# Low parts of the projection weights on another engine: GpSimd in place of DVE

## The chip, the cores and the metric

The kernel runs on one core of one Trainium2 chip. The core has five engines that matter here, each with an instruction stream of its own that it works off in order: TensorE (PE in the profile; its weight loads are PEld), VectorE (DVE), ScalarE (ACT), GpSimd (POOL) and SyncE (SP), which issues most of the transfers from device memory. The metric is the device time of one execution in microseconds (us). The kernel before was timed three times: 902.83, 899.54 and 899.51 us, median 899.54 us.

## The reference, cut to what matters

One block of a transformer for 512 tokens of width 1024, in fp32: `h = h + mixer(rmsnorm(h))`, then attention to 256 memory rows, then a gated feed-forward, then a last norm. The mixer is where the change lies. It projects the normed input `u` (512 x 1024) with one wide weight matrix and feeds three attention branches:

```
p = split_columns(u @ w_in)
o_a = stick_breaking(q_a, k_a, v_a)                                  # 4 heads
o_b = dsa(rope(q_b), rope(k_b), v_b, rope(q_idx), rope(k_idx), w_idx)  # top 128 of the keys
o_c = nsa(rope(q_c), rope(k_cmp), v_cmp, rope(k_sel), v_sel, rope(k_win), v_win, gates, ...)
g = sigmoid(g_merge)
merged = g[0]*(o_a @ w_up[0]) + g[1]*(o_b @ w_up[1]) + g[2]*(o_c @ w_up[2])
```

## The kernel before, in words

**Products in two parts.** TensorE works on a rounded form of fp32. To come near full fp32 the kernel writes each operand as a sum of a high part (the value rounded, made by a cast) and a low part (what the rounding left, made by a subtraction), and sums three products: high by high, low by high, high by low (`mm3`, L94 to L96). Every weight tile is therefore loaded by SP into a tile `raw` (128 x 1024 at most), cast on ACT into `whi` (L58), and subtracted into `wlo = raw - whi` (L66). `ring` (L71 to L87) makes such a loader for a pool: `load_split` has three buffers of each tile and subtracts on DVE, `load_fill` has two and subtracts on GpSimd. Both subtractions stand on the same line, L66, and are told apart in the profile by the engine.

**Stages.** The order in time is: the norm and the projections of branch a (0 to 54 us of the profiled execution); the stick-breaking heads of branch a (54 to 106 us), in which TensorE fills its waits with matmuls of three merge gates (tiles `gf`); the later projections (106 to 195 us); the attentions of branches c and b with the top-k search on DVE (195 to 300 us); the merge gates, the memory attention and the feed-forward.

**The later projections.** `project` (L231) is called five times: for 256 columns of keys and values of branch c (`post_g2`, two weight tiles of 4 x 256 columns), for 336 columns in three pieces (`post_g1`, weight tiles of 1008, 1008 and 672 columns), and for the queries of the indexer, of branch c and of branch b (`post_q`, two weight tiles each; in the texts below qi, qc and qb). That is eleven weight tiles. For each of four chunks of 128 tokens it accumulates 24 matmuls into a bank `gm`, ACT copies the bank to `p` (L228), and DVE applies the rotary embedding with `p` and a table `cst` (L244 to L246). For the keys GpSimd makes a second copy of each rotated row (`rk`, L299) and copies value columns (L458 to L461, L445, L446). For the queries ACT casts the rotated rows into `stk` and DVE subtracts their low part into `stk` as well (L58, L66). TensorE then transposes `rk` or `stk` (L253, L466) one or two chunks later: these transposes are put into a list `late` and issued after the matmuls of a following chunk. Between qi and qc, and between qc and qb, stand the matmuls of a compression (tiles `av`), whose weights come through `load_fill`.

**What sets the order.** The program is written as one sequence, and a scheduler in the tile layer then orders the instructions of each engine by its own estimates. On the chip each engine takes its list in order: an instruction that waits holds up all that stand behind it on the same engine. The order is thus fixed before the run, and a change of engine can move other instructions too.

Of the kernel before, what the change touches and what calls it, by code (L numbers as in the profile page):

```python
# [18 lines left out]
NK = D // P  # L19
# [7 lines left out]
def block_kernel(ctx: ExitStack, tc: tile.TileContext, A, out, dbg=None):  # L27
    nc = tc.nc
# [42 lines left out]
    def ring(pl, bufs, hi_eng=None, lo_eng=None):  # L71

        def load(shape, parts, lo_eng=lo_eng):
            n = shape[0] * shape[1]
            raw = pl.tile([P, WT], F32, name="raw", bufs=bufs[0])
            rv = raw[:, :n].rearrange("p (k n) -> p k n", n=shape[1])
            off = 0
            for src in parts:
                w = src.shape[-1]
                nc.sync.dma_start(rv[:, :, off:off + w], src)  # L80
                off += w
            hi = pl.tile([P, WT], F32R, name="whi", bufs=bufs[1])
            lo = pl.tile([P, WT], F32R, name="wlo", bufs=bufs[1])
            split(hi[:, :n], lo[:, :n], raw[:, :n], hi_eng, lo_eng)
            return [t[:, :n].rearrange("p (k n) -> p k n", n=shape[1]) for t in (hi, lo)]
        return load

    load_split = ring(stage, (3, 3))
# [14 lines left out]
    def col_view(w, c0, n):  # L103
        return w.rearrange("(k p) n -> p k n", p=P)[:, :, c0:c0 + n]
# [62 lines left out]
    def load_half(ranges, k0, kn, load):  # L167
        hi, lo = load((kn, sum(w for _, w in ranges)), [col_view(w_in, c0, w)[:, k0:k0 + kn, :] for c0, w in ranges])
        return [(hi[:, k, :], lo[:, k, :]) for k in range(kn)]
# [52 lines left out]
    def project_chunk(c, n, tiles, post, keep=0):  # L222
        acc = gm_ps.tile([P, 512], F32, name=up_tag[gm_ps is gf_ps])
        for k in range(NK):
            ins = mm3(acc[:, :n], (uT[0][:, k, cc(c)], uT[1][:, k, cc(c)]), tiles[k], k == 0, k == NK - 1)
        flush(ins, keep)
        p = pw.tile([P, 336], F32, name="p", bufs=2)
        nc.scalar.copy(p[:, :n], acc[:, :n])  # L228
        late.append(post(c, p))

    def project(ranges, kstep, post, keep=0):  # L231
        n = sum(w for _, w in ranges)
        tiles = [t for k0 in range(0, NK, kstep) for t in load_half(ranges, k0, min(kstep, NK - k0), load_split)]
        for c in range(NT):
            project_chunk(c, n, tiles, post, keep)

# [261 lines left out]
    def compressed(hid):  # L498
# [23 lines left out]
        nc.vector.tensor_copy(vc, res[0:32, 64:128])  # L522

    project([(1732, 256)], 4, post_g2)
    project([(1024, 128), (1408, 68), (1988, 140)], 3, post_g1)
    blk = [blocks_of(cmp_t[0], A["cmp_pos_k"][0]), blocks_of(cmp_t[1], A["cmp_pos_v"][0])]
    hid = av_ps.tile([P, 2, P], F32, name="av")
    project([(1152, 256)], 4, post_q(qi, 1.0), 1)
    compress(0, blk[0], A["cmp_w1_k"][0], hid)
    project([(1476, 256)], 4, post_q(qc, 0.125), 1)  # L530
# [395 lines left out]
```

## Time and profile before

| what | value |
|---|---|
| median of the three timed runs | 899.54 us |
| profiled execution | 898.28 us, its span 896.5 us |
| TensorE busy | 856.3 us, 96% of the span |
| DVE busy | 507.8 us, 57% |
| ACT busy | 411.5 us, 46% |
| GpSimd busy | 140.7 us, 16% |
| granted TensorE clock, mean | 0.994 of full speed |

The profile comes from one execution that took 898.28 us, 1.26 us less than the median of the timed runs; 1.78 us of it lie outside the profiled span. Start times are counted from the span's start. A row of the timeline gives the start, the duration, the engine, the line, the operation, the tiles (output, arrow, inputs), their shapes, a count where equal instructions are drawn together, and in brackets the idle time ahead of it with what ended that. Line numbers are those of the kernel before; behind L233 the changed kernel's are higher by 2.

### The profile page before, as it was taken

How to read it: one execution, taken by the hardware profiler on the slowest of the kernel's cores; microseconds unless marked ns; L12 is line 12 of the kernel's file. 1: busy time of each engine (PE TensorE's matmuls, PEld its weight loads, DVE VectorE, ACT ScalarE, POOL GpSimd, SP SyncE). 2: the span in 40 equal slices, each digit the busy share in tenths (PEclk: the TensorE clock that was granted, in tenths of full speed). 3: DMA queues.
4: the chain of work that ended last, by engine and by line, in shares of the span. 5: the costliest groups of instructions: out<-in, count | busy, mean ns of one | idle time of the engine just before them, and what ended most of it. 6: DMA issues, size and time to landing. Idle time of an engine off the chain costs nothing.

```text
span 896.5 us, 13084 instructions
## 1 busy us (share of the span) xinstructions
PE 856.3 (96%) x5012; PEld 731.7 (82%) x5012; DVE 507.8 (57%) x1155; ACT 411.5 (46%) x779; POOL 140.7 (16%) x116
## 2 busy tenths in 40 slices
PE   5999999899989999999989999999999999999995
PEld 5987899787757788978878979988888888888884
DVE  4456378799998305676677758643443334322226
ACT  6487545557774224544654545432322333211123
POOL 4021232302211347430232010000000000000002
PEclk9999999999999999999999999999999999999998
DMA  9340124510210334558446514642333332333312
GB/s 323 85 110 24 43 58 119 141 48 24 70 26 24 95 94 141 187 174 246 125 150 199 165 49 142 187 142 94 97 102 105 97 94 94 118 94 95 99 42 94
DMA packets 93710, 99.00 MB, mean 110 GB/s; under 512 B 4656, under 2 KB 81616, under 8 KB 93648
## 3 DMA queue, kind: packets, MB, share of 16 engines
q1 hardware_dynamic: 91568, 92.75, 34.0%
q10 hardware_dynamic: 2080, 5.42, 1.9%
q8 instruction: 39, 0.64, 0.3%
q14 instruction: 23, 0.19, 0.1%
HBM read 96.06 MB, written 2.10 MB: 109 GB/s over the span
## 4 chain that ended last, share of the span: by engine, by line
PE 85%; DVE 7%; ACT 4%; issue 2%; DMA 1%; POOL 0%; ACTq 0%; DVEq 0%; POOLq 0%
PE wo L95 9%; PE wo L96 9%; PE wo L94 9%; PE gf L94 6%; PE gf L95 6%; PE gf L96 6%; PE ff L94 4%; PE ff L95 4%; PE ff L96 4%; PE gm L94 3%; PE gm L95 3%; PE gm L96 3%; PE y L96 2%; PE y L94 2%; PE y L95 2%; PE av L101 2%
## 5 line engine op out<-in xcount | busy, mean ns | idle before, releaser
L58 ACT CAST whi<-raw 128x1024 fp32r<-128x1024 f32 (+1 forms) x167 | 174.8, 1048 | 292.4 <-PE y L96 78.9
L66 DVE TENSOR_TENSOR wlo<-raw,whi 128x1024 fp32r<-128x1024 f32 (+1 forms) x131 | 164.1, 1255 | 211.2 <-ACT whi L58 210.9
L66 POOL TENSOR_TENSOR wlo<-raw,whi 128x1024 fp32r<-128x1024 f32 x36 | 88.9, 2474 | 312.9 <-ACT whi L58 267.1
L95 PE MATMUL wo<-ut_lo,whi 128*128 128x256 f32 (+1 forms) x320 | 105.2, 329 | 0.0
L96 PE MATMUL wo<-ut_hi,wlo 128*128 128x256 f32 (+1 forms) x320 | 104.6, 327 | 0.0
L94 PE MATMUL wo<-ut_hi,whi 128*128 128x256 f32 (+1 forms) x320 | 104.4, 326 | 0.0
L96 PE MATMUL gf<-ut_hi,wlo 128*128 128x512 f32 (+1 forms) x192 | 69.8, 363 | 0.0
L94 PE MATMUL gf<-ut_hi,whi 128*128 128x512 f32 (+1 forms) x192 | 69.3, 361 | 0.0
L95 PE MATMUL gf<-ut_lo,whi 128*128 128x512 f32 (+1 forms) x192 | 69.3, 361 | 0.0
L94 PE MATMUL ff<-ut_hi,whi 128*128 128x512 f32 (+1 forms) x192 | 67.9, 354 | 0.0
L95 PE MATMUL ff<-ut_lo,whi 128*128 128x512 f32 (+1 forms) x192 | 67.9, 354 | 0.0
L96 PE MATMUL ff<-ut_hi,wlo 128*128 128x512 f32 (+1 forms) x192 | 67.9, 354 | 0.0
L95 PEld LDWEIGHTS wo<-ut_lo,whi 128*128 128x128 f32 x320 | 60.9, 190 | 6.2 <-issue 1.0
L94 PEld LDWEIGHTS wo<-ut_hi,whi 128*128 128x128 f32 x320 | 60.8, 190 | 5.8 <-issue 0.7
L96 PEld LDWEIGHTS wo<-ut_hi,wlo 128*128 128x128 f32 x320 | 60.8, 190 | 5.6 <-issue 0.4
L875 POOL TENSOR_TENSOR ut_hi<-ut_hi,ut_lo 128x512 f32<-128x512 f32 x4 | 5.0, 1276 | 367.0 <-ACT ut_hi L874 367.0
L94 PE MATMUL gm<-whi,ut_hi 128*128 128x256 f32 (+1 forms) x160 | 47.4, 296 | 0.0
L95 PE MATMUL gm<-wlo,ut_hi 128*128 128x256 f32 (+1 forms) x160 | 46.4, 290 | 0.0
L96 PE MATMUL gm<-whi,ut_lo 128*128 128x256 f32 (+1 forms) x160 | 46.3, 289 | 0.0
L96 PEld LDWEIGHTS gf<-ut_hi,wlo 128*128 128x128 f32 x192 | 36.2, 188 | 5.6 <-issue 1.2
L95 PEld LDWEIGHTS gf<-ut_lo,whi 128*128 128x128 f32 x192 | 36.2, 188 | 5.4 <-issue 0.8
L94 PEld LDWEIGHTS gf<-ut_hi,whi 128*128 128x128 f32 x192 | 36.2, 188 | 5.3 <-issue 0.8
(329 smaller groups left out, 2027.7 us busy)
## 6 DMA issues: line engine op xcount, KB each, us to landing
raw<-in_w_ffn_in_dram SPq DMA_DIRECT2D x56, 512.0 KB, 3.6
raw<-in_w_in_dram SPq DMA_DIRECT2D x46, 512.0 KB, 3.9
raw<-in_w_ffn_out_dram SPq DMA_DIRECT2D x22, 512.0 KB, 3.5
raw<-in_w_out_dram SPq DMA_DIRECT2D x16, 512.0 KB, 3.6
raw<-in_w_up_dram SPq DMA_DIRECT2D x8, 512.0 KB, 4.0
xt<-in_x_dram SPq DMA_DIRECT2D x4, 512.0 KB, 9.0
raw<-in_w_mem_kv_dram SPq DMA_DIRECT2D x4, 512.0 KB, 3.8
raw<-in_w_mem_q_dram SPq DMA_DIRECT2D x4, 512.0 KB, 3.8
```

The costliest lines, as they stand in the source:

```text
L58: nc.scalar.copy(dst, src)
L66: (lo_eng or nc.vector).tensor_sub(dst_lo, src, dst_hi.bitcast(F32))
L94: nc.tensor.matmul(dst, lh, rh, start=first, stop=False, skip_group_check=True)
L95: nc.tensor.matmul(dst, lh, rl, start=False, stop=False, skip_group_check=True)
L96: return nc.tensor.matmul(dst, ll, rh, start=False, stop=last, skip_group_check=True).ins
L101: nc.tensor.matmul(dst[64 * x:64 * x + 64], lhs[x], rhs[x], start=first, stop=last, skip_group_check=True)
L875: nc.gpsimd.tensor_mul(yo[:, n], yo[:, n], gain[:, n])
```

## The change

`project` gets its weight tiles through a loader that is `load_split` with the subtraction on GpSimd. The three buffers, the casts on ACT and the transfers stay. The other users of `load_split` keep DVE.

```
+    load_proj = lambda *a: load_split(*a, lo_eng=nc.gpsimd)
+
     def project(ranges, kstep, post, keep=0):
         n = sum(w for _, w in ranges)
-        tiles = [t for k0 in range(0, NK, kstep) for t in load_half(ranges, k0, min(kstep, NK - k0), load_split)]
+        tiles = [t for k0 in range(0, NK, kstep) for t in load_half(ranges, k0, min(kstep, NK - k0), load_proj)]
         for c in range(NT):
             project_chunk(c, n, tiles, post, keep)
```

Eleven instructions leave DVE's list and eleven enter GpSimd's. SP's list is the same. TensorE's list differs only in where some `gf` matmuls stand among those of the stick-breaking heads; from the first later projection on it is the same. ACT's list differs at two places, where instructions change places with near neighbours.

GpSimd's list at the end of branch a's projections, before. `wlo_1124`, `wlo_1157` and `wlo_1190` belong to the three merge gates that fill the stick-breaking stage, `wlo_2022` and `wlo_2052` to the first compression:

```order
L66 TENSOR_TENSOR wlo_136<-raw_133,whi_135 128x1024
L66 TENSOR_TENSOR wlo_142<-raw_139,whi_141 128x1024
L66 TENSOR_TENSOR wlo_1124<-raw_1121,whi_1123 128x1024
L66 TENSOR_TENSOR wlo_1157<-raw_1154,whi_1156 128x1024
L66 TENSOR_TENSOR wlo_1190<-raw_1187,whi_1189 128x1024
L66 TENSOR_TENSOR wlo_2022<-raw_2019,whi_2021 128x1024
```

The same place now. `wlo_1267` and `wlo_1273` are the tiles of `post_g2`, `wlo_1507` is the first of `post_g1`:

```order
L66 TENSOR_TENSOR wlo_136<-raw_133,whi_135 128x1024
L66 TENSOR_TENSOR wlo_142<-raw_139,whi_141 128x1024
L66 TENSOR_TENSOR wlo_1267<-raw_1264,whi_1266 128x1024
L66 TENSOR_TENSOR wlo_1273<-raw_1270,whi_1272 128x1024
L66 TENSOR_TENSOR wlo_1124<-raw_1121,whi_1123 128x1024
L66 TENSOR_TENSOR wlo_1157<-raw_1154,whi_1156 128x1024
L66 TENSOR_TENSOR wlo_1507<-raw_1502,whi_1506 128x1008
L66 TENSOR_TENSOR wlo_1190<-raw_1187,whi_1189 128x1024
```

Two subtractions stand ahead of the first two gates' and one behind them.

GpSimd's list where `post_g2` ends and `post_g1` begins, before (copies for the fourth chunk of `post_g2`):

```order
L299 COPY rk_1433<-rk_1433 128x64
L458 COPY vv_1489<-p_1478 128x64
L459 COPY vv_1489<-p_1478 128x64
L461 COPY vsel_1241<-p_1478 128x64
L299 COPY rk_1480<-rk_1480 128x64
L299 COPY rk_1492<-rk_1492 128x64
```

The same place now, with the second and third tile of `post_g1` (`wlo_1515`, `wlo_1523`):

```order
L301 COPY rk_1433<-rk_1433 128x64
L66 TENSOR_TENSOR wlo_1515<-raw_1510,whi_1514 128x1008
L460 COPY vv_1489<-p_1478 128x64
L461 COPY vv_1489<-p_1478 128x64
L463 COPY vsel_1241<-p_1478 128x64
L66 TENSOR_TENSOR wlo_1523<-raw_1518,whi_1522 128x672
L301 COPY rk_1480<-rk_1480 128x64
L301 COPY rk_1492<-rk_1492 128x64
```

The three copies stand between the two subtractions, and the last two copies behind both.

GpSimd's list from the end of `post_g1` to the second compression (`wlo_2266`, `wlo_2296`), before:

```order
L299 COPY rk_1714<-rk_1714 128x64
L299 COPY rk_1723<-rk_1723 128x64
L445 COPY vb_1240<-p_1774 128x64
L446 COPY vwin_1242<-p_1774 128x64
L299 COPY rk_1776<-rk_1776 128x64
L299 COPY rk_1785<-rk_1785 128x64
L299 COPY rk_1794<-rk_1794 128x64
L66 TENSOR_TENSOR wlo_2266<-raw_2263,whi_2265 128x1024
```

The same place now, with the tiles of qi (`wlo_1840`, `wlo_1846`), of qc (`wlo_2082`, `wlo_2088`) and the first of qb (`wlo_2411`):

```order
L301 COPY rk_1714<-rk_1714 128x64
L66 TENSOR_TENSOR wlo_1840<-raw_1837,whi_1839 128x1024
L301 COPY rk_1723<-rk_1723 128x64
L66 TENSOR_TENSOR wlo_1846<-raw_1843,whi_1845 128x1024
L447 COPY vb_1240<-p_1774 128x64
L448 COPY vwin_1242<-p_1774 128x64
L301 COPY rk_1776<-rk_1776 128x64
L66 TENSOR_TENSOR wlo_2082<-raw_2079,whi_2081 128x1024
L301 COPY rk_1785<-rk_1785 128x64
L301 COPY rk_1794<-rk_1794 128x64
L66 TENSOR_TENSOR wlo_2088<-raw_2085,whi_2087 128x1024
L66 TENSOR_TENSOR wlo_2411<-raw_2408,whi_2410 128x1024
```

Three subtractions stand among the `rk` copies that TensorE's transposes read, and two ahead of the second compression's. The last moved one, `wlo_2417` of qb, stands behind `wlo_2296`.

## Rows read from the trace of the kernel before

**Rows 1.** The page's first part: busy time and share of each engine.
```profile
PE 856.3 (96%) x5012; PEld 731.7 (82%) x5012; DVE 507.8 (57%) x1155; ACT 411.5 (46%) x779; POOL 140.7 (16%) x116
```
**Rows 2.** The page's fourth part: engines on the chain that ended last.
```profile
PE 85%; DVE 7%; ACT 4%; issue 2%; DMA 1%; POOL 0%; ACTq 0%; DVEq 0%; POOLq 0%
```
**Rows 3.** Busy time by stretch: length, engines, clock, DMA share, GB/s.
```profile
134.00:146.00 12.00, 11.19 (x90) 10.55 (x89) 11.98 (x45) 6.31 (x16) 3.24 (x6) 1.00 0.31 90
146.00:158.00 12.00, 12.00 (x127) 12.00 (x126) 9.05 (x19) 7.59 (x13) 3.98 (x2) 1.00 0.46 137
...
260.00:270.00 10.00, 6.87 (x42) 4.37 (x41) 9.73 (x33) 6.44 (x15) 2.37 (x1) 0.93 0.20 53
```
**Rows 4.** DVE by line and shape, 40 to 196 us: busy us, mean ns, idle before.
```profile
L66 DVE TENSOR_TENSOR wlo<-raw,whi 128x1024 fp32r<-128x1024 f32 x11 | 13.4, 1223 | 2.5 <-ACT whi L58 2.5
...
L66 DVE TENSOR_TENSOR wlo<-raw,whi 128x1008 fp32r<-128x1008 f32 x2 | 3.7, 1853 | 1.2 <-ACT whi L58 1.2
```
**Rows 5.** GpSimd in order of time, 80 to 160 us.
```profile
82.44 2.56 POOL L66 TENSOR_TENSOR wlo<-raw,whi 128x1024 fp32r<-128x1024 f32 x1 [26.77 <-ACT whi L58]
...
119.26 0.23 POOL L461 COPY vsel<-p 128x64 f32<-128x64 f32 x1
...
133.91 1.10 POOL L299 COPY rk<-rk 128x64 f32<-128x64 f32 x1 [0.51 <-DVE rk L246]
...
154.02 4.81 POOL L66 TENSOR_TENSOR wlo<-raw,whi 128x1024 fp32r<-128x1024 f32 x2 [14.55 <-ACT whi L58]
```
**Rows 6.** DVE in order of time, 54 to 161 us.
```profile
54.24 2.49 DVE L66 TENSOR_TENSOR wlo<-raw,whi 128x1008 fp32r<-128x1008 f32 x1 [0.64 <-ACT whi L58]
56.77 0.42 DVE L66 TENSOR_TENSOR ka_lo<-ps,ka_hi 128x256 fp32r<-128x256 f32 x1
...
59.01 0.69 DVE L60 CAST sph<-sbs 128x512 fp32r<-128x512 f32 x2
...
83.71 1.38 DVE L60 CAST sph<-sbs 128x128 fp32r<-128x128 f32 x1
...
144.20 0.42 DVE L66 TENSOR_TENSOR stk<-t,stk 128x256 fp32r<-128x256 f32 x1
...
156.49 2.48 DVE L245 TENSOR_TENSOR t<-p,cst 128x128 f32<-128x128 f32 x1
158.90 0.28 DVE L244 TENSOR_TENSOR t<-p,cst 128x128 f32<-128x128 f32 x1
...
160.36 0.43 DVE L66 TENSOR_TENSOR stk<-t,stk 128x256 fp32r<-128x256 f32 x1 [0.53 <-ACT stk L58]
```
**Rows 7.** TensorE in order of time, 57 to 171 us.
```profile
57.25 0.33 PE L96 MATMUL ps<-qa_hi,ka_lo 128*128 128x128 f32 x1 [0.71 <-DVE ka_lo L66]
...
119.86 0.31 PE L95 MATMUL gm<-wlo,ut_hi 128*128 128x336 f32 x1
...
121.35 0.42 PE L95 MATMUL gm<-wlo,ut_hi 128*128 128x336 f32 x1
...
135.06 0.33 PE L253 MATMUL ps<-cst,rk 128*128 128x128 f32 x1 [0.35 <-POOL rk L299]
...
145.41 0.60 PE L253 MATMUL ps<-cst,stk 128*128 128x128 f32 x4
...
161.57 0.60 PE L253 MATMUL ps<-cst,stk 128*128 128x128 f32 x4
...
170.26 0.66 PE L253 MATMUL ps<-cst,stk 128*128 128x128 f32 x4 [1.46 <-DVE stk L66]
```
**Rows 8.** ACT in order of time, 46 to 153 us.
```profile
46.88 1.05 ACT L58 CAST whi<-raw 128x1024 fp32r<-128x1024 f32 x1 [0.65 <-PE gf L96]
...
116.76 1.03 ACT L58 CAST whi<-raw 128x1008 fp32r<-128x1008 f32 x1
...
132.37 1.05 ACT L58 CAST whi<-raw 128x1024 fp32r<-128x1024 f32 x1
...
152.58 0.41 ACT L58 CAST stk<-t 128x256 fp32r<-128x256 f32 x1 [1.68 <-DVE t L246]
```

## The prediction

> **What bounds the kernel now.** I read the page's busy shares first: TensorE is busy 96% of the span, DVE 57%, GpSimd 16% [rows 1]. On shares alone GpSimd has room and DVE does not need any. The chain that ended last agrees: 85% of it is TensorE, 7% DVE and nothing to speak of GpSimd [rows 2]. So TensorE's list, taken in order, sets the time, and a change counts by what it adds to or takes from TensorE's waits. A share is a mean over stages, so the busy times by stretch come next: from 134 to 146 us DVE is busy 11.98 of 12 us, while TensorE works 11.19 [rows 3]. There the two run neck and neck, and it is in the middle of the stage that is changed. Last I read the timelines of DVE, GpSimd, TensorE and ACT through 46 to 175 us [rows 5 to 8], for who ends whose wait and by how much.
>
> **What one moved subtraction costs.** A 128 x 1024 subtraction takes 1.22 us on DVE [rows 4] and 2.40 us on GpSimd (two in 4.81 us, the row at 154.02) [rows 5]. Eight of 1024 columns, two of 1008 and one of 672 move. DVE is rid of 8 x 1.22 + 3.7 + 0.8 = 14.3 us (0.8 being 1.22 x 672/1024). GpSimd gets 2.40 x (8 x 1024 + 2 x 1008 + 672)/1024 = 25.5 us. Neither sum is on TensorE's path by itself.
>
> The two engines do not run freely beside each other. The rotary product at 156.49 us, with both inputs in SBUF, took 2.48 us, and the next of the same shape 0.28 us; it lay beside the second GpSimd subtraction of the pair 154.02 to 158.83 and ended with it [rows 5, 6]. The cast of 128 columns at 83.71 us took 1.38 us and ended where GpSimd's subtraction of 82.44 ended, at 85.0 [rows 5, 6]. The other way round, the 64-column copy on GpSimd at 133.91 took 1.10 us [rows 5], where the like of it takes 0.23 (119.26). So I count a moved subtraction as 2.40 us in which DVE's rotary products, low parts of `stk` and SBUF casts stand still, against 1.22 us of DVE work saved: a loss of 1.18 us for DVE wherever it has no idle time. Between two subtractions one DVE instruction gets through, as in the pair at 154.02.
>
> The Trainium skill, page "SBUF — State Buffer", section "Who interferes with whom", has this as a rule: a DVE instruction with two SBUF inputs contends with a GpSimd instruction that reads SBUF, and whoever issues first blocks the other fully. By that rule, the trace agrees, the blocked terms below count in full; if the two merely shared the port, only the waits for the low parts themselves would be left, which is the first rival.
>
> **Term 1, the start of the stick-breaking heads.** TensorE waits 0.71 us at 57.25 for `ka_lo` [rows 7]. `ka_lo` came only at 56.77 because the 1008-column subtraction of 54.24 to 56.73 stood ahead of it on DVE, twice its length beside GpSimd's gates [rows 6]. That goes: -0.71. Late next is the cast of `sph` at 59.01 [rows 6]. GpSimd now has five subtractions in a row from 47.93 (46.88 + 1.05, the end of the first cast [rows 8]), to 47.93 + 5 x 2.40 = 59.9 us. The cast waits until then, 0.9 us or more. TensorE, 0.71 earlier, would want it at about 59.3 and gets it at about 60.3: +1.0. Net +0.3; bounds -0.7 (the cast slips in) and +0.6 (another DVE instruction goes between two subtractions).
>
> **Term 2, the second and third tile of `post_g1`.** The cast of the second ends at 117.79 [rows 8], its subtraction on GpSimd at 117.79 + 2.36 = 120.15. TensorE wants it at 119.86 [rows 7]: +0.3. Three copies of 0.23 us stand between [rows 5], then the third tile's 1.58 us: 120.15 + 0.7 + 1.58 = 122.4 at the earliest, against 121.35 [rows 7]; where each copy lets a rotary product through first, 122.8 to 123.1. Bounds +1.05 and +1.75, I take +1.4; the 0.3 is inside it.
>
> **Term 3, qi.** The first cast ends at 133.42 [rows 8], the subtraction at 135.82, and only behind it comes the copy of `rk_1723`, to about 136.15. TensorE's transpose had it at 135.06 [rows 7]: +1.1. Behind it DVE, without idle time here [rows 3], is blocked by `wlo_1840`, `wlo_1846` and `wlo_2082`: 3 x 2.40 = 7.2 us, less the two subtractions that it made itself before this point, 2.4: 4.8 us late. The low part of `stk` for the first transposes of qi ended at 144.20 + 0.42 = 144.62, TensorE wanted it at 145.41 [rows 6, 7], 0.8 of slack. So +4.0 at that transpose, the 1.1 included. Bounds: +1.05 if the rotary products slip in between, +5.0 if nothing does.
>
> **Term 4, qc.** `wlo_2088` and `wlo_2411` block 4.8 us; DVE is rid of three subtractions by then, 3.7 us, and 9.05 of 12 us busy leave a little room [rows 3]. Slack at the first transposes of qc is 161.57 - 160.79 = 0.8 us [rows 6, 7]. That alone is +0.3. But the two casts of the second compression stand on ACT behind the cast of `stk` that already waited 1.68 us for DVE at 152.58 [rows 8]; a late DVE makes those casts late, and their two GpSimd subtractions then fall on the rotary products of qc with less room than at 156.49. Fully late that is +3.2. Bounds 0 and +3.2, I take the middle, +1.6.
>
> **Term 5, the last transposes of qc.** TensorE waits 1.46 us at 170.26 for `stk` [rows 7], behind two DVE subtractions. One of them (`wlo_2417`) goes, 1.2 us, and blocks up to 2.4 us from GpSimd instead, +1.2 at most and -1.2 if it blocks nothing. I take +0.8, near the upper end, because the row at 156.49 blocked in full, and a little is hidden while the first product waits for its `p`.
>
> At nothing I cost the three `raw` buffers that come free later, since TensorE's waits in these stretches end on DVE, ACT or GpSimd and none on a weight transfer, and everything behind 195 us, where no instruction changed; the attentions start when qb is done, so the delay is carried to the end. If that cover failed, it would cost up to the 1.2 us by which a `raw` buffer is held longer.
>
> **Sum.** 0.3 + 1.4 + 4.0 + 1.6 + 0.8 = +8.1 us on the profiled execution of 898.28: 906.4 us. The median of the timed runs stood 1.26 us above that execution, so I forecast 907.6 us.
>
> **Rivals.**
> First, only the waits for low parts count, and DVE's products slip in between GpSimd's work. For it: one did at 154.02 to 156.5. Against: the next one stood still for 2.48 us. Terms: -0.7 + 1.05 + 1.1 = about +1.5, to 899.8, or 901 as a median.
>
> Second, not slower: DVE, at 11.98 of 12 us, is the true bound of the stage, and the work taken from it ends TensorE's waits. What would go is 0.71 at 57.25, 0.35 at 135.06 and 1.46 at 170.26 [rows 7], 2.5 us: 895.8, or 897 as a median; faster than that only if the queries' chain shortens too. It decides if GpSimd's subtractions run so early that their blocking falls into DVE's idle time. For it: DVE has three quarters of its time busy behind 146 us, not all [rows 3]. Against: the cast of qi's first tile ends at 133.42 [rows 8], 1.6 us ahead of the transpose that stands before its use [rows 7], less than one subtraction of 2.40.
>
> Third, dearer: all upper bounds, 0.6 + 1.75 + 5.0 + 3.2 + 1.2 = 11.75 us, and a lower clock on top. From 260 to 270 us, with TensorE busy 6.87 of 10, the granted clock was 0.93 [rows 3]; at that, 40 us cost 2.8 us more. 898.28 + 14.5 + 1.26 = 914.
>
> That the change does not do what it says is excluded by the lists: eleven instructions changed engine.
>
> **How the numbers follow.** The forecast has 0.60 (904 to 912 us), the first rival 0.16, the second 0.10, the third 0.14. About 0.5%, 4.5 us, is what a measurement of this kernel can tell from no change: faster is under 895.0, slower over 904.0. Slower gets the forecast and the third, 0.74. Same gets the first and half of the second, 0.21. Faster gets the other half, 0.05. The range of 900 to 915 us holds the forecast, the first rival and most of the third, and leaves out the second and a worse third.
>
> **What would show it.** Right: TensorE waits with a releaser on GpSimd at the first chunk of `post_g1` and at the transposes of the last `rk` of its third chunk; a wait of 2 us or more for `stk` at the first transposes of qi; rotary products of 2 us or more on DVE between 118 and 175 us; the 0.71 us for `ka_lo` gone. Wrong: no such long rotary product beside a moved subtraction, or TensorE's idle time from 118 to 175 us not grown by over 3 us. The whole is wrong if the projections end (about 195 us) no later than before, or if a difference arises behind them.

## The result and the profile after

The changed kernel took 909.75 us (median of 4 runs, 908.94 to 910.47), the kernel before 899.52 us in the runs beside it. The ratio is 1.0114, with a 95% interval of 1.0099 to 1.0128: slower by 10.2 us. The profiled execution's span is 908.5 us, 12.0 us more than before. Below, line numbers are the changed kernel's (2 more than before behind L233); an experiment's are its own.

The first and the fourth part of the page, to be held against [rows 1, 2]:

```profile
PE 862.6 (95%) x5012; PEld 736.2 (81%) x5012; DVE 513.2 (56%) x1144; ACT 411.0 (45%) x779; POOL 163.9 (18%) x127
...
PE 80%; DVE 9%; ACT 5%; issue 2%; DMA 2%; POOL 1%; SPq 0%; ACTq 0%; DVEq 0%; POOLq 0%
```

GpSimd gained 23.2 us of busy time (140.7 to 163.9). Its weight subtractions alone gained 25.3 (36 in 88.9 us before, 47 in 114.2 now); 25.5 were worked out. DVE was rid of eleven subtractions and 14.3 us, yet its busy time rose by 5.4 us: an instruction that stands still for GpSimd is drawn as a long one. TensorE's share of the chain fell from 85% to 80%, DVE's rose from 7% to 9%.

TensorE in order of time, those rows that begin with a wait (in brackets; what ended it behind the arrow), for [rows 7]:

```profile
59.70 0.51 PE L342 MATMUL ps<-sph,fixed 128*128 128x512 f32 x1 [1.09 <-DVE sph L60]
...
84.84 0.44 PE L342 MATMUL ps<-sph,fixed 128*128 128x128 f32 x2 [1.45 <-DVE sph L60]
...
121.89 0.42 PE L95 MATMUL gm<-wlo,ut_hi 128*128 128x336 f32 x1 [0.26 <-POOL wlo L66]
...
124.00 0.42 PE L95 MATMUL gm<-wlo,ut_hi 128*128 128x336 f32 x1 [0.45 <-POOL wlo L66]
...
125.87 0.33 PE L468 MATMUL ps<-cst,rk 128*128 128x128 f32 x1 [0.62 <-POOL rk L301]
...
139.82 0.33 PE L255 MATMUL ps<-cst,rk 128*128 128x128 f32 x1 [1.62 <-POOL rk L301]
...
152.53 0.66 PE L255 MATMUL ps<-cst,stk 128*128 128x128 f32 x4 [1.25 <-DVE stk L66]
...
171.18 0.95 PE L255 MATMUL ps<-cst,stk 128*128 128x128 f32 x4 [2.28 <-DVE stk L66]
...
181.26 0.66 PE L255 MATMUL ps<-cst,stk 128*128 128x128 f32 x4 [1.27 <-DVE stk L66]
...
186.97 0.45 PE L294 MATMUL ps<-ki_hi,qi 128*128 128x384 f32 x1 [1.78 <-ACT rel L546]
```

The wait for `ka_lo` at 57.25 is gone. Three short waits for GpSimd are new in `post_g1`, the one for the last `rk` of its third chunk grew from 0.35 to 1.62 us, and the first transposes of qi (152.53) and of qc (171.18) now wait for DVE, which they did not. The last wait of 1.78 us stood before too, in the kernel before at 176.48:

```profile
172.19 0.39 PE L292 MATMUL ps<-ki_hi,qi 128*128 128x256 f32 x1 [0.56 <-ACT qc L260]
...
176.48 0.44 PE L292 MATMUL ps<-ki_hi,qi 128*128 128x384 f32 x1 [1.78 <-ACT rel L544]
```

GpSimd in order of time:

```profile
47.37 11.99 POOL L66 TENSOR_TENSOR wlo<-raw,whi 128x1024 fp32r<-128x1024 f32 x5 [28.20 <-ACT whi L58]
...
137.01 2.37 POOL L66 TENSOR_TENSOR wlo<-raw,whi 128x1024 fp32r<-128x1024 f32 x1
139.53 0.24 POOL L301 COPY rk<-rk 128x64 f32<-128x64 f32 x1
...
143.82 2.41 POOL L66 TENSOR_TENSOR wlo<-raw,whi 128x1024 fp32r<-128x1024 f32 x1 [0.38 <-ACT whi L58]
...
157.03 4.81 POOL L66 TENSOR_TENSOR wlo<-raw,whi 128x1024 fp32r<-128x1024 f32 x2 [9.59 <-ACT whi L58]
164.37 4.79 POOL L66 TENSOR_TENSOR wlo<-raw,whi 128x1024 fp32r<-128x1024 f32 x2 [2.54 <-ACT whi L58]
```

DVE in order of time:

```profile
58.38 1.53 DVE L60 CAST sph<-sbs 128x512 fp32r<-128x512 f32 x2
...
137.06 2.40 DVE L248 TENSOR_TENSOR rk<-t,t 128x64 f32<-128x64 f32 x1
...
143.90 2.57 DVE L247 TENSOR_TENSOR t<-p,cst 128x32 f32<-128x32 f32 x2
...
157.25 2.33 DVE L246 TENSOR_TENSOR t<-p,cst 128x128 f32<-128x128 f32 x1 [0.79 <-ACT p L228]
159.50 2.48 DVE L247 TENSOR_TENSOR t<-p,cst 128x128 f32<-128x128 f32 x1
...
165.54 1.37 DVE L246 TENSOR_TENSOR t<-p,cst 128x128 f32<-128x128 f32 x1 [1.74 <-ACT p L228]
166.84 2.48 DVE L247 TENSOR_TENSOR t<-p,cst 128x128 f32<-128x128 f32 x1
```

Lay the two lists side by side. The subtraction of 137.01 ends at 139.38; DVE's sum into the last `rk`, a 64-column operation that takes 0.21 us elsewhere, starts at 137.06 and ends at 139.46; the copy of `rk` follows at 139.53 and TensorE has it at 139.82. The pair of 157.03 (the second tile of qc and the first of qb) covers two rotary products, the pair of 164.37 two more. That second pair is the compression's, which GpSimd made before the change too [rows 5]; it now comes 10.35 us later and falls on the rotary products of qc's first chunk.

Where the delay arises, from TensorE's timelines of both kernels (start of the first projection, ends of the transposes, end of the last matmul):

| place | before | after | late by | added there |
|---|---|---|---|---|
| first projection starts | 105.84 | 107.45 | 1.61 | 1.61 |
| `post_g1`, second chunk | 130.78 | 134.28 | 3.50 | 1.89 |
| `post_g1`, third chunk | 135.39 | 140.15 | 4.76 | 1.26 |
| qi, first chunk | 146.01 | 153.19 | 7.18 | 2.42 |
| qc, first chunk | 162.17 | 172.13 | 9.96 | 2.78 |
| qc, last chunk | 170.91 | 181.92 | 11.01 | 1.05 |
| qb, first chunk | 187.59 | 199.43 | 11.84 | 0.83 |
| last matmul | 885.9 | 897.9 | 12.0 | 0.2 |

All of it arises ahead of 200 us. The first row holds a difference that is not the change's: TensorE waited 1.35 us at 19.85 us in the kernel before and 0.71 us at 19.22 in the changed one, each time for a low part of branch a's projections, which the change does not touch. From there to 52 us, ahead of anything that was moved, the changed kernel's execution lay 0.64 us in front. From 52 us to the first projection it thus lost 2.25 us. Busy time by stretch of the changed kernel shows one thing more (the number ahead of the last two is the granted clock):

```profile
86.00:90.00 4.00, 4.00 (x17) 3.52 (x16) 2.13 (x4) 3.12 (x8) 0.00 (x0) 0.57 0.42 125
140.00:144.00 4.00, 4.00 (x21) 3.90 (x21) 3.66 (x18) 1.76 (x5) 2.87 (x5) 0.59 0.62 164
172.00:176.00 4.00, 4.00 (x25) 4.00 (x25) 2.48 (x8) 2.48 (x5) 0.00 (x0) 0.65 0.04 12
188.00:192.00 4.00, 4.00 (x15) 3.30 (x14) 3.58 (x6) 2.68 (x6) 0.00 (x0) 0.57 0.35 106
```

Four times the clock was for the most part at its lower level (1.2 instead of 2.4 GHz), each time behind one of the waits of 1.45, 1.62, 2.28 and 1.78 us above. In the kernel before it stayed at 1.00 there, and behind its own 1.78 us too:

```profile
140.00:144.00 4.00, 4.00 (x36) 4.00 (x35) 4.00 (x13) 2.30 (x6) 0.00 (x0) 1.00 0.04 11
172.00:176.00 4.00, 2.51 (x16) 2.24 (x16) 2.90 (x2) 1.55 (x5) 3.67 (x2) 1.00 0.46 118
176.00:180.00 4.00, 3.52 (x19) 2.95 (x19) 3.50 (x7) 2.96 (x6) 0.00 (x0) 1.00 0.55 150
```

So the span has two accounts: TensorE's waits, which between 46 and 212 us grew from 7.2 to 12.8 us, and slow matmuls. Whether the second is a cost of its own was to be tested.

### The profile page after: what moved, and what is told of

It is laid out like the page before. It is cut to its first block, busy times and chain, and to the rows that moved or that the text cites. A ratio compares the mean times of both kernels' runs of the same rounds, so it can differ in the third digit from the quotient of the medians.

```text
span 908.5 us, 13086 instructions
## 1 busy us (share of the span) xinstructions
PE 862.6 (95%) x5012; PEld 736.2 (81%) x5012; DVE 513.2 (56%) x1144; ACT 411.0 (45%) x779; POOL 163.9 (18%) x127
## 4 chain that ended last, share of the span: by engine, by line
PE 80%; DVE 9%; ACT 5%; issue 2%; DMA 2%; POOL 1%; SPq 0%; ACTq 0%; DVEq 0%; POOLq 0%
PE wo L95 9%; PE wo L96 9%; PE wo L94 8%; PE gf L94 5%; PE gf L95 5%; PE gf L96 5%; PE ff L95 4%; PE ff L94 4%; PE ff L96 4%; PE gm L94 2%; PE gm L95 2%; PE gm L96 2%; PE y L94 2%; PE y L95 2%; PE y L96 2%; PE av L101 2%
## 5 line engine op out<-in xcount | busy, mean ns | idle before, releaser
L66 DVE TENSOR_TENSOR wlo<-raw,whi 128x1024 fp32r<-128x1024 f32 x120 | 149.9, 1251 | 208.0 <-ACT whi L58 207.7
L66 POOL TENSOR_TENSOR wlo<-raw,whi 128x1024 fp32r<-128x1024 f32 (+2 forms) x47 | 114.2, 2438 | 304.7 <-ACT whi L58 250.7
```

The source lines that it names most:

```text
L66: (lo_eng or nc.vector).tensor_sub(dst_lo, src, dst_hi.bitcast(F32))
```

## The experiments

The theory: a subtraction on GpSimd makes DVE's instructions with two SBUF inputs, and its casts, stand still for its 2.4 us, and DVE's lateness reaches TensorE. The rivals: only the low parts' own lateness counts; or GpSimd's being busy is enough, whatever it does; or the clock makes a good part of the loss.

**The parts one by one.** `project` gets its loader as an argument; GpSimd's is given in one place, or two, at a time:

```
+    def project(ranges, kstep, post, keep=0, load=load_split):
...
+    project([(1152, 256)], 4, post_q(qi, 1.0), 1, load=load_proj)   # e_qi; the others alike
```

> Only the two tiles of post_g2 are subtracted on GpSimd. Theory (GpSimd's subtractions make DVE stand still, and TensorE's waits of some 1.5 us are each followed by a stretch at the lower clock): the 0.71 us wait for ka_lo goes, a wait of about 1 us for sph comes at 59, and the wait for sph at 84 keeps its 1.1 to 1.5 us; 899 us if the clock stays at its upper level from 84 to 96, 901 us if it falls there as in the changed kernel. Rival (only the waits for the low parts themselves count): these tiles are wanted 50 us later, so only the 0.71 us goes, 898.8 us.

900.42 us against 899.67, ratio 1.0008 (0.9997 to 1.0020): no difference to be told. The 0.71 us went, a wait of 0.56 us for `sph` came at 60.11, and the clock did not fall at 84; the first projection started 0.16 us later. The theory said 899 us for that case and the rival 898.8: the gain that both had did not come, because of the wait for `sph`, which is the theory's, at half its length. The run decides little.

> Only the three tiles of post_g1 are subtracted on GpSimd. Both the theory and the rival expect TensorE's waits for wlo and rk of 0.26, 0.45 and 0.62 us between 120 and 127 us, +1.3; the theory adds a shorter stall of sph at 59 (one GpSimd subtraction less in a row than with post_g2's), 0 to +0.5. 900.8 to 901.3 us. If the cost of the whole change is an interaction of its parts, this one gives no measurable difference.

901.64 us, ratio 1.0027 (1.0015 to 1.0039), with waits of 0.27 and 0.46 us for `wlo` and 0.28 for `rk`. The waits are as expected of both, the time lies 0.3 us above the range. In the heads TensorE waited 1.47 us for `sph` at 84.25, and the clock was 0.79 from 84 to 92 us, which neither had said of this run.

> Only the two tiles of qi are subtracted on GpSimd. Theory: rk on GpSimd stands behind the first subtraction, TensorE waits over 1 us for it (0.35 before), DVE is late by two locked subtractions and TensorE waits about 1 us for stk at the first transposes of qi; +2.5 us, and +1.7 more if TensorE's clock falls to its lower level behind the wait for rk: 902 to 903.7 us. Rival: the wait for rk alone, +1.1, 900.6 us, and no wait for stk at the first transposes.

901.51 us, ratio 1.0021 (1.0007 to 1.0035): 1.9 us, under what the theory said and over the rival's 900.6 us. The wait for `rk` was there in full and the clock was 0.63 from 136 to 140 us; the wait for `stk` at qi's first transposes was not, as the rival had it.

```profile
136.03 0.33 PE L255 MATMUL ps<-cst,rk 128*128 128x128 f32 x1 [1.62 <-POOL rk L301]
```

So qi's two tiles do not exhaust DVE's slack at qi; the next run shows that qc's do.

> Only the four tiles of qc and qb are subtracted on GpSimd. Theory: their low parts are never waited for, but DVE's rotary products stand still beside them: the wait for stk before the scores grows from 1.46 to over 2 us, another of about 1 us comes at the last transposes of qc, and the clock falls to its lower level once or twice behind them; +2 us at the upper clock, +3.7 to +5.4 with the lower one: 901.5 to 905 us. Rival: DVE is rid of four subtractions and nobody waits for a low part, 898 to 899.5 us.

903.43 us, ratio 1.0039 (1.0026 to 1.0052). Here the theory and the first rival are far apart: no matmul waited for one of these four low parts, and still

```profile
146.79 0.66 PE L255 MATMUL ps<-cst,stk 128*128 128x128 f32 x4 [0.79 <-DVE stk L66]
...
164.54 0.66 PE L255 MATMUL ps<-cst,stk 128*128 128x128 f32 x4 [1.39 <-DVE stk L66]
...
174.62 0.66 PE L255 MATMUL ps<-cst,stk 128*128 128x128 f32 x4 [2.81 <-DVE stk L66]
```

TensorE waited for DVE at the first transposes of qi and of qc, and longer at qc's last. The fall of the clock that I expected behind them did not come. The four ratios add up to 0.95%, the whole change cost 1.14%: within their intervals the parts add. In the profiled executions, one of each, they do not quite: qb's last transposes end 0.3, 2.8, 1.8 and 3.9 us later than in the kernel before, 8.8 us together, and 11.9 us later in the changed kernel.

**The standstill by itself.** The kernel before, DVE making the projections' low parts, and beside it work on GpSimd that nobody needs:

```
             split(hi[:, :n], lo[:, :n], raw[:, :n], hi_eng, lo_eng)
+            if extra:                       # the eleven projection tiles
+                nc.gpsimd.tensor_sub(raw[:, :n], raw[:, :n], hi[:, :n].bitcast(F32))   # e_dup
+                # e_set, instead: twice nc.gpsimd.memset(raw[:, :n], 0.0)
```

> The kernel before, in which DVE makes all low parts as it did, plus eleven subtractions of the same size on GpSimd whose results nobody reads (each writes raw - hi over raw, when DVE is done with it). No low part comes later for its own sake. Theory (GpSimd's subtraction makes DVE stand still): the waits of the changed kernel come back although DVE gives the low parts, and DVE has its 14.3 us still to do: 908 to 914 us, with rotary products of 1.2 us and more beside the added subtractions. Rival (the low parts themselves come too late): 899.5 to 901.5 us, the rest being copies of rk that stand behind an added subtraction on GpSimd.

921.01 us against 899.31, ratio 1.0239 (1.0220 to 1.0259): 21.7 us, above my range. TensorE at the first transposes of qi and at the first and the last of qc:

```profile
158.76 0.66 PE L257 MATMUL ps<-cst,stk 128*128 128x128 f32 x4 [1.82 <-DVE stk L66]
...
179.59 0.66 PE L257 MATMUL ps<-cst,stk 128*128 128x128 f32 x4 [3.06 <-DVE stk L66]
...
191.20 0.66 PE L257 MATMUL ps<-cst,stk 128*128 128x128 f32 x4 [4.32 <-DVE stk L66]
```

DVE's own low parts stood still with the rest: TensorE waited 2.15 us at 129.05 for one that DVE made, so that a low part did come late here, though not for being moved, and 1.68 and 1.66 us for `sph` in the heads. The waits for `stk` alone come to 10.4 us, and no wait ended on a weight's transfer or cast.

> The kernel before, with two memsets of raw on GpSimd (about 1 us each for 1024 columns, by the memsets at the kernel's start) in the places of the added subtractions of the run before: GpSimd is busy about as long, but writes only. Theory (DVE's second SBUF input and GpSimd's reads exclude each other): no rotary product is stretched, 900 to 902 us, the copies of rk behind a memset being late by up to 1 us. If being busy beside DVE is enough to stop it, as long as with the subtractions: 907 us and more.

900.64 us, ratio 1.0019 (1.0009 to 1.0028): 1.3 us. By line and shape, 100 to 185 us (busy, mean ns, idle before), the memsets and the rotary product here, then the same product in the kernel before and in the changed kernel:

```profile
L87 POOL MEMSET raw<- 128x1024 f32 x12 | 11.4, 953 | 16.8 <-DVE wlo L66 16.5
L249 DVE TENSOR_TENSOR t<-p,cst 128x128 f32<-128x128 f32 x18 | 6.4, 355 | 1.8 <-ACT p L231 1.8
```
```profile
L244 DVE TENSOR_TENSOR t<-p,cst 128x128 f32<-128x128 f32 x19 | 6.1, 322 | 2.1 <-ACT p L228 2.1
```
```profile
L246 DVE TENSOR_TENSOR t<-p,cst 128x128 f32<-128x128 f32 x16 | 9.3, 580 | 3.7 <-ACT p L228 3.7
```

The same rotary product took 355 ns on average beside memsets, 322 in the kernel before and 580 in the changed kernel. Sixteen memsets ran in that stretch, two to a tile, those of 1024 columns for 953 ns each. The first rival falls by the one run, the second by the other: what stops DVE is GpSimd reading SBUF, not its being busy. That is also where the Trainium skill, page "SBUF — State Buffer", section "Who interferes with whom", draws the line: a GpSimd instruction that only writes does not contend with DVE's second input. These two runs agree, with 0.19% against 2.39%.

**The clock.** The changed kernel, with TensorE kept at work in two of its waits (other functions as they were):

```
         tp = ps.tile([P, 4, P], F32, name="ps")
+        for _ in range(pad):                # 7 at post_g1's third chunk, 10 at qc's first
+            nc.tensor.matmul(tp.rearrange("p a b -> p (a b)"), uT[0][:, 0, 0:P], uT[0][:, 0, :],
+                             start=True, stop=True, skip_group_check=True)
```

> The changed kernel, with TensorE kept busy in two of its waits: 7 matmuls of 512 columns (some 1.5 us) into a tile that is overwritten, ahead of the transposes of the third chunk of post_g1 (the wait of 1.62 us for rk), and 10 of them (some 2.1 us) ahead of the first transposes of qc (the wait of 2.28 us for stk). Theory (the stretch at the lower clock follows from TensorE's wait): no stretch at the lower clock from 140 to 144 and from 172 to 176 us, 1.5 to 1.7 us less for each: 906.5 us. Rival (the clock falls for another reason, whenever it falls): both stretches stay, 909.8 us, or up to 911 where a filler outlasts its wait.

910.37 us, ratio to the kernel before 1.0128 (1.0111 to 1.0146): no gain over the changed kernel's 1.0114. And yet the lower clock did go from both places:

```profile
136.00:146.00 10.00, 9.76 (x67) 8.67 (x66) 9.97 (x27) 3.66 (x8) 8.56 (x9) 1.00 0.42 113
168.00:178.00 10.00, 9.76 (x96) 8.77 (x94) 7.52 (x18) 5.42 (x11) 3.03 (x2) 1.00 0.35 98
178.00:188.00 10.00, 6.34 (x34) 5.91 (x35) 6.79 (x13) 5.83 (x12) 4.93 (x3) 0.83 0.70 177
```

In the changed kernel the first two stretches had 0.83. The useless matmuls did not outlast their waits: the transposes of qc behind them still waited 0.20 us for `stk`. So the lower clock went, but the time did not come back. Up to the last transposes of qc the trace shows where it went:

```profile
180.77 1.11 PE L257 MATMUL ps<-cst,stk 128*128 128x128 f32 x4 [2.81 <-DVE stk L66]
```

That wait was 1.27 us in the changed kernel. A faster TensorE arrives earlier at DVE's late tile and waits there, and the clock falls behind that wait instead. From 134 to 182 us DVE's chain is the bound, and what TensorE loses to its clock there costs nothing more: these transposes end at 181.88 us here and at 181.92 in the changed kernel. My sum of 1.5 to 1.7 us a time was wrong.

Behind them e_warm did gain. Its wait for `rel` was 0.89 us instead of 1.78, the clock stayed up from 188 to 192, and qb's last transposes ended at 205.88 us instead of 207.72. The profiled execution lost 1.5 us of it at 477 us, in a stretch at the lower clock that the profiles of the other two kernels do not have there, and the timed runs show no gain either.

```profile
476.00:482.00 6.00, 4.62 (x27) 4.63 (x28) 4.91 (x12) 1.96 (x3) 0.00 (x0) 0.72 0.55 173
```

That the useless matmuls kept the clock up is likely, but one execution does not show it. In the heads, where e_warm's lists are still the changed kernel's and nothing was filled, its clock stayed up behind a wait of 1.47 us, and the changed kernel's fell behind one of 1.45:

```profile
85.65 0.44 PE L344 MATMUL ps<-sph,fixed 128*128 128x128 f32 x2 [1.47 <-DVE sph L60]
```
```profile
86.00:90.00 4.00, 4.00 (x24) 3.43 (x24) 1.36 (x3) 2.98 (x8) 0.00 (x0) 1.00 0.44 131
```

**Smaller pieces.** The changed kernel, each moved subtraction in four:

```
+                for x in range(0, n, n // 4):
+                    v = slice(x, x + n // 4)
+                    nc.gpsimd.tensor_sub(lo[:, v], raw[:, v], hi[:, v].bitcast(F32))
```

> The changed kernel, with each moved subtraction made in four pieces of a quarter of its columns (some 0.6 us each). Theory (DVE stands still for one GpSimd instruction at a time, and one DVE instruction gets through between two of them): a DVE instruction waits 0.6 us instead of 2.4, four get through beside one low part instead of one, and the chain of rotary products to the transposes is late by less: 904 to 907 us, with no rotary product over 1 us beside a moved subtraction. Rival (DVE stands until the whole low part is done, or the low parts' own lateness is what costs): 909 to 911 us.

908.72 us, ratio 1.0101 (1.0084 to 1.0118): not told apart from the whole subtractions. The mechanism was as expected: beside eight pieces (6.25 us from 157.51) DVE made five operations of 0.72 to 0.85 us each, one between any two pieces. What failed is the gain in time. From the first projection on the pieces did help: qb's last transposes came 7.1 us later by it than in the kernel before, against 10.3 in the changed kernel. But ahead of it more was lost: the first projection started at 108.57 us, 1.1 us later than in the changed kernel, with four waits of 0.2 to 0.3 us for `sph` and `spl` between 59 and 63 us. And behind the pieces the compression's pair, whole as ever, met the next products, and qc's last transposes waited 2.75 us:

```profile
164.21 2.06 DVE L252 TENSOR_TENSOR t<-p,cst 128x128 f32<-128x128 f32 x1 [1.74 <-ACT p L234]
166.19 2.48 DVE L253 TENSOR_TENSOR t<-p,cst 128x128 f32<-128x128 f32 x1
```

**The other way round.** If the standstill costs so much, subtractions that GpSimd makes in the kernel before should go to DVE.

```
+            w = load_fill((8, 128), [...], lo_eng=nc.vector)    # compression: e_cmpdve, and in the other three
+    merge_up(0, "a", lambda *a: load_fill(*a, lo_eng=nc.vector), gf_ps)    # e_cmpup, e_alldve
+    def fill_gate(j, f, n=S, load_fill=load_fill):    # e_alldve: gates 0 to 2 on DVE; e_best: 0 to 4
```

> The kernel before, with the opposite move: the low parts of the four weight tiles of the compression go from GpSimd to DVE (4 x 2.4 us off GpSimd, 4 x 1.22 us onto DVE). Theory (GpSimd's subtraction costs DVE its own 2.4 us wherever they meet): the 1.78 us wait for rel in the scores goes, since DVE's second product of the scores no longer stands still for 2.4 us; the 1.46 us wait for stk stays within 1 us; 897.5 to 898.5 us. Rival (DVE is full in this stage and every subtraction off it helps): 900 to 902 us.

898.76 us, ratio 0.9993 (0.9982 to 1.0004): the same. The wait at qc's last transposes fell from 1.46 to 0.78 us, but the wait of 1.78 us for `rel` stayed, and here the clock was 0.57 behind it, from 176 to 180 us, so that qb's last transposes ended later than before (196.52 us against 195.85). The pair on GpSimd beside the scores, at 170.31 here, was not the compression's.

> The kernel before, with the low parts of the compression's four tiles and of the first output merge's two tiles (the pair on GpSimd at 170.77 us in the kernel before, beside which the second product of the scores took 2.40 us) on DVE. Theory: DVE stands idle for 2.7 us just there and makes them in 2.4 us, the product is not stretched, the wait of 1.78 us for rel goes; with the 0.5 us at the transposes of qc that the compression's four gave: 897.0 to 898.0 us. Rival (the wait for rel has another cause, or DVE is late by its two subtractions): 898.8 us and more.

901.26 us, ratio 1.0017 (1.0006 to 1.0028). I had named the wrong tiles once more: the pair stayed, at 169.73, and so did the wait; the two that moved lay behind 260 us.

> The same, and the low parts of the first three gates' tiles on DVE too, so that GpSimd makes no subtraction of a weight tile between 46 us and the end of the projections. Theory: the cast of sph at 83.71 us is not held up and the 1.07 us wait for it goes; the subtraction of post_g1's first tile takes 1.2 us instead of 2.5 beside GpSimd's gates, but DVE makes the gates' two of 1.22 as well, so the wait of 0.71 us for ka_lo stays within 0.7: 895.5 to 897.5 us. Rival (in the heads DVE's own time is the bound): ka_lo comes later by 1 to 2 us, 898 to 900 us.

899.53 us, ratio 1.0000 (0.9990 to 1.0010). The waits for `ka_lo` and for `sph` at 84 were both gone, and qb's last transposes ended 2.81 us earlier than before (193.04 against 195.85), although the pair beside the scores (at 167.92 here) and the wait of 1.78 us for `rel` were still there. The last matmul ended no earlier (886.4 against 885.9): the gain was lost beside DVE's top-k rounds, between 268 and 288 us, where the merge's low part is now waited for:

```profile
267.53 0.50 PE L96 MATMUL gf<-o_hi,wlo 128*128 128x512 f32 x1 [0.69 <-DVE wlo L66]
```

This one wait is not all of it. But with TensorE's lists matched instruction by instruction, e_cmpup, which moves the merge's two tiles as well, lost 3.1 us in the same stretch, and e_best below, which leaves them on GpSimd, lost nothing there.

> The opposite move at five places of the kernel before: the low parts of the compression's four tiles and of the gates' tiles 0 to 4 go from GpSimd to DVE; the first output merge keeps GpSimd. The pair at 170.77 us in the kernel before belongs to gates 3 and 4, not to the output merge, as the run e_cmpup took it. Theory: the wait of 1.78 us for rel goes, since DVE, idle for 2.7 us ahead of it, makes the pair in 2.4; qb's last transposes came 2.8 us earlier in e_alldve, and what that kernel lost behind 260 us (DVE making the merge's low parts beside the top-k rounds) does not come back: 895 to 896.5 us. Rival (a wait for rel of another cause stays, and the tail takes the gain): 897.5 to 899.5 us.

895.29 us against 900.26, ratio 0.9951 (0.9938 to 0.9964): faster than both kernels. DVE ahead of the scores and in them:

```profile
167.48 2.36 DVE L66 TENSOR_TENSOR wlo<-raw,whi 128x1024 fp32r<-128x1024 f32 x2 [0.52 <-ACT whi L58]
169.76 0.48 DVE L545 SCALAR_TENSOR_TENSOR score<-rel,wi,cst 128x256 f32<-128x256 f32 x1
170.35 1.66 DVE L545 SCALAR_TENSOR_TENSOR score<-rel,wi,score 128x256 f32<-128x256 f32 x3
```

DVE makes the pair in a gap that it had anyway. Three products of the scores take 1.66 us together, where the kernel before had

```profile
172.93 0.51 DVE L545 SCALAR_TENSOR_TENSOR score<-rel,wi,cst 128x256 f32<-128x256 f32 x1 [2.73 <-ACT rel L544]
173.55 3.58 DVE L545 SCALAR_TENSOR_TENSOR score<-rel,wi,score 128x256 f32<-128x256 f32 x3
```

and the 1.78 us wait is gone. The first projection starts at 103.10 (105.84 before) and qb's last transposes end at 190.77, 5.1 us earlier; 0.6 us of that lead stood already at 52 us, ahead of the moved tiles.

## Why the prediction was right, and where it was not

The forecast was 907.6 us and came 2.2 us short of 909.75: +8.1 us were forecast, +10.2 measured as medians and 12.0 between the two profiled executions. Its mechanism, GpSimd's subtraction as time in which DVE stands still, was the one at work, and e_dup and e_set show it without the rest of the change. Of its signs, the two waits for GpSimd, the long rotary products and the end of the wait for `ka_lo` came, and TensorE's idle time from 118 to 175 us grew by 3.35 us (3.13 to 6.48), against the 3 that were asked. One sign did not come: the wait for `stk` at qi's first transposes was 1.25 us and not 2 or more.

- **What one subtraction costs.** 2.40 us as said, and 25.3 us in all for 25.5. The 14.3 us taken from DVE hold the 2.49 us of the row at 54.24, which was itself stretched; unstretched they are 13.0. DVE's operations beside it took up to 2.5 us, one getting through between two subtractions.
- **Term 1, +0.3; measured 1.61, or 2.25 from 52 us on.** The wait for `ka_lo` went and `sph` came 1.09 us late (1.0 said). I left out what lies behind it: the next wait for `sph` at 84, 1.45 instead of 1.07 us, and the lower clock from 86 to 90, behind which TensorE has no wait over 0.3 us up to the projections that could hide it. e_warm, with the same lists and waits up to there and without that fall, lost 0.90 us in the same stretch, so that the fall made about 1.35 in these two executions.
- **Term 2, +1.4 (1.05 to 1.75); measured 1.89.** The three waits make 1.33; the other 0.56 arise at the same three places, beyond what the trace lists as idle time there.
- **Term 3, +4.0; measured 3.7** (1.26 at `rk`, 2.42 from there to qi). The steps held, the copy of `rk` behind the subtraction and DVE late by three subtractions, but TensorE lost the 2.42 us only in part at the transposes where they were forecast: 1.25 us is the wait there, the rest arose ahead of it, where the clock was at 0.59. By e_qi qi's own tiles make no wait there, by e_qcqb the later ones make 0.79 us, and all together made 1.25.
- **Term 4, +1.6 (0 to 3.2); measured 2.78.** The step named in it, the compression's casts pushed back so that its pair falls on qc's rotary products, happened in full (10.35 us later, 1.37 and 2.48 us at 165.54). I took the middle of the bounds where the upper end was due.
- **Term 5, +0.8; measured 1.05, for another reason, so that its size is luck.** The wait itself shrank, from 1.46 to 1.27 us; 1.24 us arose ahead of it, between the first and the second chunk of qc, in the lower clock from 172 to 176.
- **Nothing behind the projections.** True: 0.2 us. But the scores, between qc and qb, took 0.83 us more, at the lower clock from 188 to 192. I had left them out.

So the terms that were too small are 1 and 4, by 2.0 (from 52 us on) and 1.2 us, and the missing one is the scores, 0.8. The misses did not cancel each other: all terms but the third were too small, and the measured 10.2 us lie between the forecast's 8.1 and the 11.75 of all upper bounds. The first rival (only the waits for the low parts) is refuted by e_dup and e_qcqb, the second (not slower) by the result. The third was right that the clock would fall, but its price was not: by e_warm the falls between 140 and 176 us cost nothing beyond DVE's lateness up to the last transposes of qc. The one at 86 did cost, about 1.35 us; what the one at 188 cost by itself was not tried.

## What to carry to other kernels

An engine's idle share is no room for work that stops its neighbour: price an elementwise move from DVE to GpSimd as GpSimd's own duration, in which DVE stands still wherever its next instruction reads two SBUF operands. Look for the opposite move too: work that GpSimd does beside a full DVE may take half the time in a gap that DVE already has (0.49% here), as long as DVE is not the bound there, as it was in the top-k rounds. And where TensorE waits for a late engine, fixing what TensorE lost ahead of that wait gained nothing up to it (e_warm); ask first who is late at the next meeting.

## What was not expected of the hardware

TensorE's clock fell to its lower level behind waits of 1.45, 1.62, 1.78 and 2.28 us, in a stage where the engine is otherwise busy, and stayed up in two of the places when the wait was filled with useless matmuls (e_warm). The wait's length does not decide it alone: behind the wait for `sph` at 84 to 86 us the changed kernel's clock fell and e_warm's did not, with the same lists up to there (1.45 and 1.47 us). The kernel before and e_alldve had their wait of 1.78 us without a fall, e_cmpdve had the same wait with one. And in e_g2 the clock was 0.57 from 172 to 176, behind waits of 1.47 and 0.56 us that the kernel before has too. What else decides it stays open.

Blocked time is drawn as busy time. DVE was rid of 14.3 us of drawn time and showed 5.4 us more; only the mean per shape (322 to 580 ns) tells that it stood still.
